# A two-layer encoder: the memory attention's transposes one unit later, with eight buffers of probabilities instead of four

## The chip, the cores and the metric

The kernel runs on one core of one Trainium2 chip. The metric is the device time of one execution in microseconds. The core has five engines that take their own instruction queues in order: PE (TensorE, matrix products and transposes), DVE (VectorE), ACT (ScalarE), POOL (GpSimd) and SP, which here only issues transfers. PEld is PE's weight load.

## What is computed

An encoder of two layers over 1024 positions of width 1024, in float32. Each layer has a mixing half with three groups and a gated feed-forward half. The change sits in the third group, attention of four heads of width 64 to 256 memory rows:

```python
def _memory_attn(q, km, vm):
    scores = jnp.einsum('bshd,bmhd->bhsm', q, km) * (HEAD_DIM ** -0.5)
    probs = jax.nn.softmax(scores, axis=-1)
    return jnp.einsum('bhsm,bmhd->bshd', probs, vm)

# in each layer
y = concat([rmsnorm(y_fourier), rmsnorm(y_window), rmsnorm(y_memory)]) @ w_out
x = x + rmsnorm(y)
gate, up = split(rmsnorm(x) @ w_ffn_in)
x = x + rmsnorm((silu(gate) * up) @ w_ffn_out)
```

## The kernel before, in words

**Precision.** Most products are made of float32 operands that are split in a high and a low part, and three products of the parts (`Acc.add`, L160). A split is a cast on ACT (L151) and a subtraction on DVE or POOL (L152).

**Memory attention** works in eight units, one per head and half of the sequence (512 positions). `mem_scores` (L828) multiplies queries and keys into two PSUM tiles `ms` (L839); DVE takes the row maximum (L841) and scales it (L842), ACT takes the exponential (L845) into a buffer of the ring `ems` and sums it, DVE takes the reciprocal of the sums (L849, tile `rden`), and POOL scales the probabilities in place (L851). `mem_turn` (L856) transposes them on PE into `mpT` (L861) and splits them into the ring `mps`, whose two buffers hold one unit. `mem_values` (L867) multiplies them with the values into `mav` (L872) and folds the two halves (ACT L875, DVE L876) into `ym`. One unit takes two buffers of `ems`, so its four buffers (at 16, 18, 20 and 22 of the float32 arena) hold two units.

**The order as written** (`mem_units`, L878): step i makes the scores of unit i, the values of unit i - 2 and the transposes of unit i - 1. The steps are woven by `weave` with the last query tiles (`q`, products `qp`, rotation L637, L639 on DVE and L642 on POOL; `q_turn`, transposes `qT`, split L379, L380).

**What follows it in each layer.** `fm_units` (L942) multiplies the Fourier and memory parts of each position tile with their rows of `w_out` (products `mo` from `big`). It first needs `group_scale` (L916): squares on ACT (L921) into the ring `sqs` at 16 and 18, a sum over partitions on PE (`ssp`, L924), L926 on DVE, L928 on POOL; only then can ACT and DVE empty its PSUM banks (L967, L969), of which there are two. It is woven with the first group of the window attention: scores `sc` (L727), DVE L728, exponential L740, POOL scaling L751, transposes `pT` (L764), values `av` (L779), folded into `ya` at 8 to 15 (L800, L801). Beside these, `load_wout` splits `w_out` (ACT L909, DVE L910). After that come the second group, `out` (products `mo` from `arena_r`, L1007, the norms L322 to L325 and L289), the transposes `hTp` (L1032) and the feed-forward products `qy`, `qz`, `qx`, `qw` (L1103), whose weight sums DVE makes in L1093.

**What sets the order.** The calls above are not the order of the queues. The program's builder runs its own scheduler over them (`schedule_with_timeline_sim=True` in `kernel`), which keeps data dependences and buffer reuse, and writes one in-order queue per engine. So a change of the written order changes the queues wherever the scheduler then decides otherwise.

Of the kernel before, what the change touches and what calls it, by code (L numbers as in the profile page):

```python
# [68 lines left out]
def tile_encoder(ctx: ExitStack, tc: tile.TileContext, T, C, out):  # L69
# [30 lines left out]
    def at(k, *shape, dt=F32):  # L100

        o = int(k * 256)
        ap = arenas[F32R if dt is F32R else F32][:, o : o + math.prod(shape)]
        return shaped(ap.bitcast(dt) if dt is I32 else ap, shape)
# [16 lines left out]
    def run(k, n, step):  # L121
        return Ring(*[k + i * step for i in range(n)])
# [2 lines left out]
    raws, junks = run(0, 3, 2), Ring(56)  # L125
    yfs, turns, kvs, ds = run(8, 2, 1), Ring(32, 34), Ring(10, 56, 58), run(12, 2, 2)
    ropes = {2: run(6, 4, 0.5), 8: run(36, 6, 2)}
    ems, es_ring, y1s = run(16, 4, 2), run(33, 5, 3), run(6, 2, 1)
    sqs, pms, xfs = run(16, 2, 2), run(20, 2, 2), Ring(16, 20, 24, 28, 32, 0)
    qws, sns, silus, acts = Ring(32, 0, 16, 20), Ring(36, 38, 40, 42, 32, 34), run(8, 5, 2), run(18, 7, 2)  # L130
    sums, wsums = run(8, 4, 2), Ring(4, 6)
# [327 lines left out]
    class Mix:  # L459
# [418 lines left out]
        def mem_units(self):  # L878
            todo = [(h, half) for half in range(2) for h in range(4)]
            st, pp = {}, {}  # L880
            n = len(todo)

            def unit(i):
                if i < n:
                    st[i] = self.mem_scores(*todo[i])
                if i >= 2:
                    h, half = todo[i - 2]
                    if h == 0 and half == 0:
                        ym = at(24, 2, 2, 512)
                        self.ym = [ym[:, i] for i in range(2)]  # L890
                    self.mem_values(h, half, pp.pop(i - 2))
                if 1 <= i <= n:
                    pp[i - 1] = self.mem_turn(st.pop(i - 1))

            return [lambda i=i: unit(i) for i in range(n + 2)]


        def load_wout(self, ks, k0=None):
# [424 lines left out]
    for l in range(DEPTH):  # L1323
# [57 lines left out]
        st = {}  # L1381
# [85 lines left out]
```

## Time and profile before

| | us |
|---|---|
| median of 3 runs (lowest to highest) | 2129.55 (2124.32 to 2131.04) |
| the profiled execution: its own time | 2127.03 |
| its span, first to last instruction | 2125.2 |
| PE busy | 2008.2 (94%) |
| DVE busy | 1594.6 (75%) |
| ACT busy | 1068.3 (50%) |
| POOL busy | 862.9 (41%) |

The span is the profiled execution without some 2 us around it. The shares are means over stages: the feed-forward half is nearly all PE, and what PE loses it loses in short stretches. The memory attention lies at about 139 to 224 us in layer 0 and 1185 to 1266 us in layer 1, the feed-forward half starts at about 406 and 1447 us.

### The profile page before, as it was taken

The numbers are of one execution on the slowest core, as the hardware profiler recorded it, in microseconds if no ns is written. First come the engines' busy times: TensorE is split into PE (matmuls) and PEld (weight loads), VectorE is DVE, ScalarE is ACT, GpSimd is POOL, SyncE is SP. The second block draws the span as 40 slices with busy tenths as digits, with TensorE's granted clock in tenths as the row PEclk, the third lists the DMA queues.
The fourth block names the chain that finished last, engine by engine and source line by source line (L and its number), as shares of the span: only waits on it lengthen the run. The fifth ranks groups of instructions, "written<-read, shape, count | busy, mean of one in ns | idle before, by whom it ended". The sixth has DMA issues, their size and how long they took to land. (4 is left out here: it accounts for less than half of the span.)

```text
span 2125.2 us, 28513 instructions
## 1 busy us (share of the span) xinstructions
PE 2008.2 (94%) x9586; PEld 1655.2 (78%) x9586; DVE 1594.6 (75%) x2445; ACT 1068.3 (50%) x2269; POOL 862.9 (41%) x858
## 2 busy tenths in 40 slices
PE   7998999699999999999899979997999999989997
PEld 6886787488888887888778868775888888877885
DVE  7568666998877877667967686669887877877674
ACT  6477767553333334444545676775333333345441
POOL 4234437643423434321544444576443423432222
PEclk9999999899999999999999989998999999999998
DMA  6112122422332326987721122142332332389872
GB/s 222 45 50 65 65 95 106 152 65 95 122 100 94 111 95 193 352 270 263 257 84 45 49 70 99 67 143 95 104 109 95 119 100 93 119 290 328 278 229 79
DMA packets 173603, 287.52 MB, mean 135 GB/s; under 512 B 15480, under 2 KB 73360, under 8 KB 173456
## 3 DMA queue, kind: packets, MB, share of 16 engines
q1 hardware_dynamic: 165392, 266.82, 37.9%
q10 hardware_dynamic: 8064, 18.88, 2.3%
q8 instruction: 75, 1.23, 0.2%
q14 instruction: 72, 0.59, 0.1%
HBM read 219.06 MB, written 66.58 MB: 134 GB/s over the span
## 5 line engine op out<-in xcount | busy, mean ns | idle before, releaser
L151 ACT CAST arena_r<-arena_f 128x512 fp32r<-128x512 f32 (+1 forms) x780 | 444.6, 592 | 679.8 <-PE qz L1103 116.4
L152 DVE TENSOR_TENSOR arena_r<-arena_f,arena_r 128x512 fp32r<-128x512 f32 x676 | 545.2, 829 | 173.8 <-ACT arena_r L151 170.2
L1234 PE MATMUL fo<-arena_r 128*128 128x512 f32 x1848 | 437.5, 398 | 28.4 <-ACT arena_r L151 15.2
L1234 PEld LDWEIGHTS fo<-arena_r 128*128 128x128 f32 x1848 | 354.1, 193 | 106.9 <-ACT arena_r L151 17.8
L1103 PE MATMUL qy<-arena_r 128*128 128x512 f32 x1056 | 264.0, 399 | 27.8 <-ACT arena_r L151 22.9
L1103 PEld LDWEIGHTS qy<-arena_r 128*128 128x128 f32 x1056 | 202.7, 193 | 73.6 <-ACT arena_r L151 24.0
L1093 DVE TENSOR_TENSOR arena_f<-arena_f 128x512 f32<-128x512 f32 x220 | 204.6, 933 | 5.1
L1103 PE MATMUL qz<-arena_r 128*128 128x512 f32 x704 | 196.0, 389 | 0.2 <-DVE arena_r L152 0.2
L1123 POOL TENSOR_TENSOR arena_f<-arena_f 128x512 f32<-128x512 f32 x44 | 73.1, 1660 | 294.5 <-ACT arena_f L1108 294.5
L1215 POOL TENSOR_TENSOR arena_f<-arena_f 128x512 f32<-128x512 f32 x50 | 72.5, 1454 | 229.4 <-DMA arena_f<-in_w_ffn_out 145.0
L1103 PEld LDWEIGHTS qz<-arena_r 128*128 128x128 f32 x704 | 132.0, 188 | 28.0 <-DVE arena_r L152 0.7
L1155 POOL TENSOR_TENSOR arena_f<-arena_f 128x512 f32<-128x512 f32 x44 | 73.5, 1672 | 173.4 <-DVE arena_f L1135 126.3
L152 POOL TENSOR_TENSOR arena_r<-arena_f,arena_r 128x256 fp32r<-128x256 f32 (+2 forms) x104 | 84.1, 813 | 126.9 <-ACT arena_r L151 95.0
L1103 PE MATMUL qw<-arena_r 128*128 128x512 f32 x528 | 127.6, 389 | 0.8 <-ACT arena_r L151 0.8
L1103 PE MATMUL qx<-arena_r 128*128 128x512 f32 x528 | 127.7, 389 | 0.5 <-ACT arena_r L151 0.5
L1103 PE MATMUL qx<-big,arena_r 128*128 128x512 f32 x528 | 127.0, 389 | 0.0
L1103 PEld LDWEIGHTS qw<-arena_r 128*128 128x128 f32 x528 | 99.1, 188 | 21.8 <-ACT arena_r L151 1.2
L1103 PEld LDWEIGHTS qx<-arena_r 128*128 128x128 f32 x528 | 99.1, 188 | 21.4 <-ACT arena_r L151 0.9
L1103 PE MATMUL qz<-big,arena_r 128*128 128x512 f32 x352 | 115.5, 389 | 0.0
L1103 PEld LDWEIGHTS qx<-big,arena_r 128*128 128x128 f32 x528 | 99.1, 188 | 20.5
L162 PE MATMUL mo<-arena_r 128*128 128x512 f32 x384 | 102.2, 403 | 3.2 <-DVE arena_f L1007 3.2
L162 PE MATMUL mo<-big,arena_r 128*128 128x512 f32 x384 | 102.9, 407 | 0.3 <-ACT arena_f L967 0.3
(225 smaller groups left out, 3570.6 us busy)
## 6 DMA issues: line engine op xcount, KB each, us to landing
arena_f<-in_w_ffn_out SPq DMA_DIRECT2D x264, 256.0 KB, 4.3
arena_f<-in_w_ffn_in SPq DMA_DIRECT2D x88, 512.0 KB, 3.6
actd<-arena_f SPq DMA_DIRECT2D x154, 256.0 KB, 3.7
arena_f<-actd SPq DMA_DIRECT2D x154, 256.0 KB, 4.1
arena_f<-in_w_in SPq DMA_DIRECT2D x40, 256.0 KB, 2.7
arena_f<-in_x SPq DMA_DIRECT2D x16, 512.0 KB, 5.0
arena_f<-in_w_out SPq DMA_DIRECT2D x32, 256.0 KB, 2.7
pmd<-arena_f ACTq DMA_DIRECT2D x32, 256.0 KB, 2.0
```

Source lines behind the costliest of these rows:

```text
L151: nc.scalar.copy(hi, src)
L152: return (lo_eng or nc.vector).tensor_tensor(out=lo, in0=src, in1=f32(hi), op=ALU.subtract)
L162: mm(self.dst, a, b, start=self.i == 0, stop=self.i == self.n - 1)
L1093: nc.vector.tensor_tensor(out=s, in0=a, in1=b, op=op)
L1103: mm(pt, a, b, start=start and n == 0, stop=n == 11, skip_group_check=not start)
L1123: nc.gpsimd.tensor_tensor(out=self.v, in0=self.v, in1=self.s2, op=ALU.add)
L1155: (G if i in (0, 3) else V).tensor_tensor(out=a[i], in0=c, in1=g[i], op=ALU.mult)
L1215: (nc.vector, nc.gpsimd)[k % 2].tensor_tensor(out=s, in0=x, in1=y, op=op)
L1234: mm(pt, ab[:, 0, x, sl], ab[:, 1, y], start=new and first and j == 0, stop=last and j == 2, skip_group_check=not new)
```

## The change

The transposes of a unit are called two steps behind its scores instead of one, its values three instead of two, and `ems` gets four more buffers, at 8, 10, 12 and 14. There are eleven steps instead of ten, so `weave` mixes them a little differently with the query tiles.

```diff
-    ems, es_ring, y1s = run(16, 4, 2), run(33, 5, 3), run(6, 2, 1)
+    ems, es_ring, y1s = Ring(16, 18, 20, 22, 8, 10, 12, 14), run(33, 5, 3), run(6, 2, 1)
...
             def unit(i):
                 if i < n:
                     st[i] = self.mem_scores(*todo[i])
-                if i >= 2:
-                    h, half = todo[i - 2]
-                    if h == 0 and half == 0:
+                if i >= 3:
+                    h, half = todo[i - 3]
+                    if i == 3:
                         ym = at(24, 2, 2, 512)
                         self.ym = [ym[:, i] for i in range(2)]
-                    self.mem_values(h, half, pp.pop(i - 2))
-                if 1 <= i <= n:
-                    pp[i - 1] = self.mem_turn(st.pop(i - 1))
+                    self.mem_values(h, half, pp.pop(i - 3))
+                if 2 <= i < n + 2:
+                    pp[i - 2] = self.mem_turn(st.pop(i - 2))
 
-            return [lambda i=i: unit(i) for i in range(n + 2)]
+            return [lambda i=i: unit(i) for i in range(n + 3)]
```

Lines behind L884 stand one further down in the changed kernel. No instruction is added or taken away; the queues of all engines are permuted between the memory attention and the first feed-forward products of each layer, and are equal elsewhere. Three places follow, as they stand in the built programs.

**PE, layer 0, behind the memory attention**, from a sum over partitions on. `mav_2108` is the last unit's values, `sc` and `pT` belong to the window attention, and `mo_2187` is the product of `fm_units` that follows its first two. Before:

```order
L924 MATMUL ssp_2312<-const,arena_f 128x2 x2
L779 MATMUL av_2216<-arena_r 128x512
L764 MATMUL pT_2320<-const,arena_f 128x128 x4
L727 MATMUL sc_2476<-arena_r 128x384 x2
L764 MATMUL pT_2329<-const,arena_f 128x128 x4
L764 MATMUL pT_2338<-const,arena_f 128x128 x4
L162 MATMUL mo_2187<-big_2064,arena_r 128x512 x3
L162 MATMUL mo_2187<-big_2071,arena_r 128x512 x3
L727 MATMUL sc_2576<-arena_r 128x384 x2
```

Now:

```order
L925 MATMUL ssp_2157<-const,arena_f 128x2 x2
L872 MATMUL mav_2108<-arena_r 128x512
L727 MATMUL sc_2252<-arena_r 128x384 x2
L727 MATMUL sc_2352<-arena_r 128x384 x2
L925 MATMUL ssp_2209<-const,arena_f 128x2 x2
L727 MATMUL sc_2356<-arena_r 128x384 x2
L727 MATMUL sc_2360<-arena_r 128x384 x2
L162 MATMUL mo_2187<-big_2043,arena_r 128x512 x3
L162 MATMUL mo_2187<-big_2050,arena_r 128x512 x3
L727 MATMUL sc_2364<-arena_r 128x384 x2
L764 MATMUL pT_2217<-const,arena_f 128x128
```

The product `mo_2187` stood behind 18 transposes `pT`, four `av` and five pairs of `sc` that follow the last `mav`; now it stands ahead of the first `pT`, and the transposes come among the products.

**DVE, layer 1, around the reciprocal of the fourth unit** (`rden_10210` before, `rden_10189` now). L637 and L639 rotate the last query tile. Before:

```order
L842 TENSOR_SCALAR nmx_10190<-rmax_10189 128x2
L380 TENSOR_TENSOR arena_r<-qT_10265,arena_r 64x4x128
L910 SCALAR_TENSOR_TENSOR big_10510<-arena_f,const,big_10510 128x512
L876 TENSOR_TENSOR arena_f<-mav_10216,arena_f 64x512
L152 TENSOR_TENSOR arena_r<-mpT_10230,arena_r 128x512
L637 TENSOR_TENSOR arena_f<-qp_10370,const 128x512
L639 TENSOR_TENSOR arena_f<-qp_10370,const 128x512
L841 TENSOR_REDUCE rmax_10274<-ms_10277 128x2
L849 RECIPROCAL rden_10210<-den_10191 128x4
```

Now:

```order
L911 SCALAR_TENSOR_TENSOR big_10489<-arena_f,const,big_10489 128x512
L152 TENSOR_TENSOR arena_r<-mpT_10250,arena_r 128x512
L849 RECIPROCAL rden_10189<-den_10170 128x4
L876 TENSOR_TENSOR arena_f<-mav_10243,arena_f 64x512
L152 TENSOR_TENSOR arena_r<-mpT_10257,arena_r 128x512
L637 TENSOR_TENSOR arena_f<-qp_10349,const 128x512
L639 TENSOR_TENSOR arena_f<-qp_10349,const 128x512
L911 SCALAR_TENSOR_TENSOR big_10489<-arena_f,const,big_10489 128x512
L841 TENSOR_REDUCE rmax_10216<-ms_10219 128x2
L380 TENSOR_TENSOR arena_r<-qT_10292,arena_r 64x4x128
```

The reciprocal moved ahead of the rotation, and one split of `w_out` (L910, now L911) and one split of `qT` (L380) moved behind it. On POOL the scaling of this unit stands behind the rotation's last step, L642, in both.

**DVE, layer 0, where the feed-forward half starts.** L1093 (now L1094) is the first sum of feed-forward weights. Before:

```order
L324 SCALAR_TENSOR_TENSOR arena_f<-arena_f,rrs_3984 128x1024
L1050 TENSOR_TENSOR arena_f<-big_3511,big_3504 128x512
L1050 TENSOR_TENSOR arena_f<-big_3504,big_4003 128x512
L1007 SCALAR_TENSOR_TENSOR arena_f<-mo_4025,grs_3950,arena_f 128x512
L152 TENSOR_TENSOR arena_r<-big_4003,arena_r 128x4x128
L1007 SCALAR_TENSOR_TENSOR arena_f<-mo_4039,grs_3950,arena_f 128x512
L152 TENSOR_TENSOR arena_r<-arena_f,arena_r 128x4x128
L1093 TENSOR_TENSOR arena_f<-arena_f 128x512
```

Now:

```order
L1008 SCALAR_TENSOR_TENSOR arena_f<-mo_4039,grs_3950,arena_f 128x512
L289 SCALAR_TENSOR_TENSOR arena_f<-arena_f,nrs_3993 128x1024
L324 SCALAR_TENSOR_TENSOR arena_f<-arena_f,rrs_4057 128x1024
L1051 TENSOR_TENSOR arena_f<-big_3504,big_4003 128x512
L152 TENSOR_TENSOR arena_r<-big_4003,arena_r 128x4x128
L1064 TENSOR_TENSOR big_3996<-big_3996,big_4003 128x4x128
L325 TENSOR_TENSOR arena_f<-arena_f 128x1024
L152 TENSOR_TENSOR arena_r<-arena_f,arena_r 128x4x128
L1094 TENSOR_TENSOR arena_f<-arena_f 128x512
```

Five more instructions of DVE now stand ahead of the first weight sum: one each of L289, L324, L325, L152 and L1063. They stood behind it before.

## Rows read from the trace of the kernel before

**Rows 1.** Busy time by stretch, layer 0; PEclk is the granted clock's share.

```profile
183.00:203.00 20.00, 14.50 (x65) 11.10 (x64) 19.26 (x33) 16.45 (x41) 8.14 (x13) 0.83 0.40 128
203.00:224.00 21.00, 15.02 (x81) 11.54 (x80) 17.96 (x49) 15.78 (x45) 9.44 (x17) 0.92 0.08 26
224.00:235.00 11.00, 9.79 (x47) 8.43 (x46) 5.98 (x24) 9.17 (x27) 5.21 (x9) 0.73 0.01 1
...
241.00:350.00 109.00, 108.72 (x604) 88.98 (x603) 67.21 (x186) 72.54 (x192) 52.64 (x83) 1.00 0.28 98
...
397.00:431.00 34.00, 17.56 (x63) 12.74 (x62) 32.78 (x41) 16.35 (x29) 16.04 (x13) 0.70 0.39 123
```

**Rows 2.** The same view, layer 1.

```profile
1229.00:1258.00 29.00, 20.58 (x93) 14.44 (x92) 27.35 (x49) 23.31 (x60) 15.43 (x21) 0.86 0.30 95
1258.00:1272.00 14.00, 11.24 (x56) 9.09 (x55) 10.46 (x35) 10.27 (x28) 3.10 (x7) 0.87 0.00 1
```

**Rows 3.** PE in order of time, layer 0: start, duration, instruction, idle and releaser.

```profile
216.83 0.71 PE L861 MATMUL mpT<-const,arena_f 128*128 128x128 f32 x5
...
224.46 0.51 PE L924 MATMUL ssp<-const,arena_f 128*128 128x2 f32 x4
...
232.97 1.91 PE L764 MATMUL pT<-const,arena_f 128*128 128x128 f32 x8
234.53 2.28 PE L162 MATMUL mo<-big,arena_r 128*128 128x512 f32 x6
```

**Rows 4.** ACT in order of time, layer 0.

```profile
212.64 0.42 ACT L921 ACTIVATE arena_f<-arena_f 128x256 f32<-128x256 f32 x1 [0.61 <-PE mpT L861]
...
230.97 0.67 ACT L967 ACTIVATE arena_f<-mo,grs 128x512 f32<-128x512 f32 x1
...
232.06 0.37 ACT L800 COPY arena_f<-av 64x256 f32<-64x256 f32 x1
```

**Rows 5.** PE in order of time at full clock, layer 0.

```profile
249.50 0.60 PE L764 MATMUL pT<-const,arena_f 128*128 128x128 f32 x4
249.85 0.48 PE L779 MATMUL av<-arena_r 128*128 128x512 f32 x1
250.17 1.55 PE L162 MATMUL mo<-big,arena_r 128*128 128x512 f32 x6
...
258.45 0.50 PE L924 MATMUL ssp<-const,arena_f 128*128 128x2 f32 x4
258.81 1.00 PE L727 MATMUL sc<-arena_r 128*128 128x384 f32 x4
```

**Rows 6.** PE in order of time, layer 1: the longest stall in the memory attention.

```profile
1234.41 1.85 PE L861 MATMUL mpT<-const,arena_f 128*128 128x128 f32 x8 [2.45 <-POOL arena_f L851]
```

**Rows 7.** POOL in order of time, just ahead of that stall.

```profile
1232.18 1.27 POOL L642 TENSOR_TENSOR arena_f<-arena_f 128x512 f32<-128x512 f32 x1 [7.03 <-DVE arena_f L639]
1233.43 2.29 POOL L851 TENSOR_SCALAR arena_f<-arena_f,rden 128x256 f32<-128x256 f32 x4
```

**Rows 8.** DVE in order of time, the same place.

```profile
1227.86 0.68 DVE L380 TENSOR_TENSOR arena_r<-qT,arena_r 64x512 fp32r<-64x512 f32 x1
1228.58 0.75 DVE L910 SCALAR_TENSOR_TENSOR big<-arena_f,const,big 128x512 fp32r<-128x512 f32 x1
...
1230.76 0.68 DVE L637 TENSOR_TENSOR arena_f<-qp,const 128x512 f32<-128x512 f32 x1
1231.36 0.68 DVE L639 TENSOR_TENSOR arena_f<-qp,const 128x512 f32<-128x512 f32 x1
```

**Rows 9.** DVE in order of time, layer 0, the feed-forward half's start.

```profile
404.99 0.68 DVE L1093 TENSOR_TENSOR arena_f<-arena_f 128x512 f32<-128x512 f32 x1
...
409.08 1.27 DVE L289 SCALAR_TENSOR_TENSOR arena_f<-arena_f,nrs 128x1024 f32<-128x1024 f32 x1
...
410.88 1.27 DVE L324 SCALAR_TENSOR_TENSOR arena_f<-arena_f,rrs 128x1024 f32<-128x1024 f32 x1
...
412.67 1.21 DVE L325 TENSOR_TENSOR arena_f<-arena_f 128x1024 f32<-128x1024 f32 x1
```

**Rows 10.** PE in order of time, layer 0, its first feed-forward product.

```profile
406.38 1.22 PE L1103 MATMUL qy<-arena_r 128*128 128x512 f32 x2 [8.88 <-ACT arena_r L151]
```

## The prediction

> **What bounds the kernel now.** I read the page's slices first, for where PE falls below nine tenths, and then the busy times of the four main engines in those stretches. In layer 0 PE is busy 14.50 of 20 us from 183 on, 15.02 of the next 21 and 9.79 of the next 11, and the granted clock falls to 0.83, 0.92 and 0.73 of full speed, that is, part of the time stands at the lower of its two levels [rows 1]. In layer 1 it is busy 20.58 of 29 us and 11.24 of 14 [rows 2]. Idle PE time in these stretches sums to 12.7 us in layer 0 and 11.2 us in layer 1; busy time multiplied by the missing share of the clock gives 6.3 and 4.3 us more. That is 34.5 us, the ceiling of anything that a change to the memory attention can return.
>
> The column beside it says why so little of it is free. DVE is busy 19.26 of the first 20 us, 17.96 of the next 21, and in layer 1 27.35 of 29 [rows 1, 2]. It splits transposed probabilities, takes maxima and splits `w_out` all at once. PE's gaps there are DVE's work seen from the other side; a new order can only return what DVE idles: 0.7 and 3.0 us in layer 0, then 5.0 us from 224 to 235, and 1.7 and 3.5 us in layer 1.
>
> From 241 us on PE is full at full clock for 109 us, with DVE at 67.21 [rows 1]. So time won before 241 us is kept until the feed-forward half starts. There DVE binds again, 32.78 of 34 us, while PE is busy 17.56 [rows 1].
>
> **The change part by part.** The written delay is mostly not what changes. In the built programs PE takes the transposes of a unit behind the scores of the next one both before and now: the scheduler had already moved them. The pairs of units, their counts and the products that PE has issued are the same until the memory attention's last third in layer 0, and nearly so in layer 1. What changes is where the neighbours stand.
>
> *The four buffers, and their new places.* They add no instruction. Two things could wait for them. The first write of `ya`, which now overlaps the last two units' probabilities, must follow their transposes: those start last at 216.83, the write comes at 232.06, 15 us of cover [rows 3, 4]. If the cover went, DVE's first fold and the first `y` split would be late next, and PE would have `mo` to do. The other direction is the gain: the squares for the first position tile reuse buffers 16 and 18, and at 212.64 they waited for PE's transposes [rows 4]. With eight buffers these places are left by the fifth unit and not by the seventh. I cost the buffers at nothing and book their gain with the next item.
>
> *Layer 0, 183 to 224 us.* The same products in nearly the same order against a DVE that idles 3.7 us. I take 1.5 us: the fourth unit's reciprocal and its scaling come a few instructions earlier, and one or two score maxima move behind the point where PE resumes `mo`. Ends: nothing, and 3.7 us.
>
> *Layer 0, 224 to 235 us, the largest term.* The first sum over partitions stood at 224.46, so ACT could empty the first `mo` bank only at 230.97, and `mo` resumed at 234.53 [rows 3, 4]. Between, PE had 18 transposes, 4 `av`, 3 sums and 5 pairs of `sc`. At full clock these cost 0.35 us per four transposes, 0.32 per `av`, 0.36 per sum and at most 0.50 per pair [rows 5]: 1.6 + 1.3 + 1.1 + 2.5 = 6.5 us, in 10.1 us of time. So 3.6 us were lost to waits for POOL's and DVE's small steps and to the lower clock; eight transposes alone took 1.91 us there [rows 3]. Now the sums stand ahead of these, and `mo`, which waits for none of this, stands ahead of and among the transposes. I take 3.0 of the 3.6 us. Ends: a loss of 1, if the sums still come late on POOL, and 4.5, if the clock also recovers earlier before 241.
>
> *Layer 1.* The longest stall is 2.45 us, transposes of the fourth unit that wait for POOL's scaling [rows 6]. The reciprocal now stands five instructions of DVE earlier, some 3.4 us by the durations of 0.68 to 0.75. But POOL's queue has the rotation's last step, L642, ahead of the scaling, before and now, and L642 waited for DVE's L639 [rows 7, 8]. So the scaling can come earlier only as L639 does: by the L910 and the L380 that moved behind it, 0.75 + 0.68 = 1.4 us [rows 8]. I take 1.5 us for the whole layer, since here `mo` resumes at much the same place as before. Ends: a loss of 1, and the 5.2 us that DVE idles.
>
> *The start of the feed-forward half.* In layer 0 five instructions of DVE move ahead of the first weight sum: 1.27 + 1.27 + 1.21 for L289, L324 and L325, and L152 and L1063 at 0.68 each like L1093 [rows 9], together 5.1 us. The first product waited 8.88 us for the casts behind that sum [rows 10], so it will come later by up to that much; but the five are then done, the last tiles' transposes come sooner, and the products that follow wait less. DVE is full either way. I take zero. Ends: 1.2 us gained, what DVE idles there, and 5.1 lost. The transfers of `x`, `pmd` and the weights keep their number and, in pairs, their order; nothing is booked for them.
>
> *A rule against this reading.* The row shows DVE at 19.26 of 20 us in PE's bubbles [rows 1]. The Trainium skill (Perfetto Trace Analysis, Optimization Strategy) says that a gap which repeats on the engine that should be full can mean too few buffers for the next tile. By the rows the sum stays as it is; by that rule the eight buffers would close the gaps, which is the third rival.
>
> **The sum:** 1.5 + 3.0 + 1.5 + 0 = 6.0 us. The profiled execution took 2127.03 us, so 2121.0 us. It lies 2.5 us under the median of the three runs, 2129.55, whose spread is 6.7 us; I keep 2121.0. For this kernel 0.3% (6.4 us, about what a measurement can tell from no change) puts the bounds at 2123.2 and 2135.9.
>
> **The rivals.** *DVE gives nothing back.* For: it is full in three of the five stretches and full again at the feed-forward start, where an earlier arrival only meets DVE's own backlog. Against: PE is full for 109 us between, with DVE at 62%, so DVE has time to catch up. Then only a part of the second term stays: about 2 us, 2125 to 2131.
>
> *Slower: the later first weight sum in layer 0.* The five instructions delay the first feed-forward product by 5.1 us, PE stands idle longer, and its clock, already 0.70 there [rows 1], returns later: at that level 17.56 us of busy time lose 5.3 us now, and half as much again is 2.6. With nothing won upstream that is 2127.0 + 7.7 = 2134.7, with a little lost there 2137. It decides if the products that follow the first do not wait less than before by as much as the first waits more. For: DVE has 1.2 us of slack in 34. Against: the same five must be done for those products in any order.
>
> *The buffers were the limit.* If scores could run ahead and fill PE, as the rule has it, half the ceiling of 34.5 us would come back: 2110. Against: the number of score products ahead of the transposes is unchanged in the queue.
>
> *The change doesn't do what it says.* As to the written delay this is so already, and it is in the sum; with no side effect at all it is the first rival.
>
> **How the numbers follow.** The forecast gets 0.53 (2114 to 2125), DVE's backlog 0.29, the slower case 0.13, the buffers 0.05. Of the forecast 0.43 lies below 2123.2 and 0.10 above; with the third rival that makes 0.48 faster; 0.10 and 0.29 with 0.01 of the slower case make 0.40 the same, and 0.12 slower. The range leaves out the buffers and about half of the slower case: 2112 to 2135. The ends of the four terms, -3.7 to 0, -4.5 to 1, -5.2 to 1 and -1.2 to 5.1, reach 2112.4 and 2134.1, so it takes them in.
>
> **What would show it.** In the changed profile the second square's wait should end far before 212, the first emptied `mo` bank should come before 226 in layer 0, and PE should be busy over 10 of the 11 us from 224 at a clock of 0.85 or more, with the same products done some 4 us earlier at 241. In layer 1 the stall of 2.45 us should shrink to about 1. The first feed-forward product of layer 0 should wait longer than 8.88 us, and the ones behind it less. I am wrong if the layer-0 gain before 241 is under 2 us, or if PE's last feed-forward transposes come later than before by more than was won.

## The result, and the profile after

| | before | after |
|---|---|---|
| median, us (runs) | 2127.39 (12) | 2134.81 (12) |
| lowest to highest | 2124.32 to 2131.04 | 2131.45 to 2138.94 |
| the profiled execution | 2127.03 | 2134.53 |

The ratio is 1.0033, with a 95% interval of 1.0024 to 1.0042: the change costs 7.4 us. The forecast was 6.0 us less than before. All twelve runs of the kernel after lie above the slowest run of before.

From the page of the kernel after, the engines' busy times (share of the span, instructions):

```profile
PE 2007.6 (94%) x9586; PEld 1653.5 (78%) x9586; DVE 1598.3 (75%) x2445; ACT 1064.2 (50%) x2269; POOL 851.2 (40%) x858
```

PE's busy time is 0.6 us less than before and the span 7.5 us longer (2132.7), so all of the loss is idle time of PE. The stretches of [rows 1], in the kernel after (window, us, then each engine's busy time, PEclk, DMA share, GB/s):

```profile
183.00:203.00 20.00, 15.13 (x66) 11.30 (x65) 17.42 (x30) 15.20 (x38) 7.62 (x11) 0.74 0.41 133
203.00:224.00 21.00, 16.45 (x74) 11.17 (x73) 17.99 (x45) 16.36 (x44) 5.76 (x11) 0.87 0.12 37
224.00:235.00 11.00, 11.00 (x49) 9.49 (x48) 7.42 (x26) 7.54 (x21) 7.32 (x13) 0.79 0.14 50
241.00:350.00 109.00, 107.88 (x604) 87.99 (x602) 69.06 (x192) 73.36 (x198) 53.34 (x80) 1.00 0.27 95
397.00:431.00 34.00, 16.26 (x61) 12.72 (x61) 30.34 (x34) 16.40 (x30) 14.08 (x13) 0.70 0.42 139
```

In the first three stretches PE idles 4.87 + 4.55 + 0 = 9.4 us, where it idled 12.7. The granted clock is lower in the first two. Busy time multiplied by its missing share is 3.93 + 2.14 + 2.31 = 8.4 us, where it was 6.3. So in this execution 3.3 us of gaps are closed, and the lower clock costs 2.1 us more. How much of this another execution would show is told in the section on the prediction.

The stretches of [rows 2], moved by 3 us, since the memory attention of layer 1 starts 3.3 us later (its first scores at 1188.36 against 1185.06):

```profile
1232.00:1261.00 29.00, 19.08 (x93) 15.35 (x93) 26.71 (x48) 23.88 (x59) 10.48 (x18) 0.80 0.30 93
1261.00:1275.00 14.00, 11.17 (x57) 8.21 (x57) 10.92 (x34) 8.81 (x25) 3.70 (x9) 0.93 0.00 1
```

Here nothing is won: PE idles 9.92 + 2.83 = 12.8 us instead of 11.2, and busy time by missing clock is 4.6 us instead of 4.3.

PE in order of time in the kernel after (start, duration, instruction, idle and releaser), beside [rows 3], [rows 6] and [rows 10]:

```profile
226.91 2.40 PE L162 MATMUL mo<-big,arena_r 128*128 128x512 f32 x6
...
229.50 0.38 PE L764 MATMUL pT<-const,arena_f 128*128 128x128 f32 x2
...
401.47 1.94 PE L1033 MATMUL hTp<-const,arena_f 128*128 128x128 f32 x8 [6.14 <-DVE arena_f L289]
412.56 1.22 PE L1104 MATMUL qy<-arena_r 128*128 128x512 f32 x2 [9.14 <-ACT arena_r L151]
...
422.30 5.07 PE L1104 MATMUL qy<-arena_r 128*128 128x512 f32 x14 [4.07 <-ACT arena_f L1109]
...
1239.72 2.07 PE L872 MATMUL mav<-arena_r 128*128 128x512 f32 x4 [3.18 <-DVE arena_r L152]
...
1245.52 1.14 PE L861 MATMUL mpT<-const,arena_f 128*128 128x128 f32 x4 [2.87 <-POOL arena_f L851]
```

`mo` resumes at 226.91 and not at 234.53, ahead of the transposes `pT`, as read from the queues. At the start of the feed-forward half PE waits 6.14 us for the transposes of a late position tile, then 9.14 for the first weights. From 385 to 431 us it idles 19.4 us, all in the three idles shown; before it idled 17.9 us there, 8.88 of them in one piece. In layer 1 the longest stalls of the memory attention were 2.45 and 1.75 us, now they are 3.18 and 2.87.

To see where the 7.4 us are lost, take one instruction late in each layer's start, DVE's fourth difference of gated products (L1124, now L1125). Before:

```profile
489.60 0.69 DVE L1124 TENSOR_TENSOR arena_f<-qy,arena_f 128x512 f32<-128x512 f32 x1
...
1529.55 0.69 DVE L1124 TENSOR_TENSOR arena_f<-qy,arena_f 128x512 f32<-128x512 f32 x1
```

After:

```profile
492.59 0.69 DVE L1125 TENSOR_TENSOR arena_f<-qy,arena_f 128x512 f32<-128x512 f32 x1
...
1535.66 0.68 DVE L1125 TENSOR_TENSOR arena_f<-qy,arena_f 128x512 f32<-128x512 f32 x1
```

The first scores of layer 0 start at 139.13 before and 138.59 after, so layer 0 loses 2.99 + 0.54 = 3.5 us up to there. Layer 1 starts 3.30 us late and is 6.11 late at its landmark: 2.8 more. The last product ends 7.5 us late. These are two single executions; the last section shows that the landmark of layer 0 differs by 3 us and more between equal queues. The shares below therefore come from ratios of many runs.

### The profile page after: what moved, and what is told of

Its sections match the earlier page's. It is cut to its first block, busy times and chain, and to the rows that moved or that the text cites. A ratio compares the mean times of both kernels' runs of the same rounds, so it can differ in the third digit from the quotient of the medians.

```text
span 2132.7 us, 28503 instructions
## 1 busy us (share of the span) xinstructions
PE 2007.6 (94%) x9586; PEld 1653.5 (78%) x9586; DVE 1598.3 (75%) x2445; ACT 1064.2 (50%) x2269; POOL 851.2 (40%) x858
## 4 chain that ended last, share of the span: by engine, by line
PE 72%; DVE 10%; DMA 7%; ACT 4%; POOL 3%; issue 3%; SPq 0%; DVEq 0%; POOLq 0%; ACTq 0%
PE fo L1235 12%; PE qz L1104 11%; PE qx L1104 11%; PE qy L1104 10%; PE mo L162 6%; PE qw L1104 5%; DVE arena_r L152 4%; PE kvp L162 4%; PE qp L162 3%; DMA arena_f<-actd 3%; DMA arena_f<-in_w_ffn_out 2%; PE pT L764 2%; PE sc L727 2%; ACT arena_r L151 1%; PE zT L162 1%
## 5 line engine op out<-in xcount | busy, mean ns | idle before, releaser
L152 DVE TENSOR_TENSOR arena_r<-arena_f,arena_r 128x512 fp32r<-128x512 f32 x676 | 545.3, 828 | 182.4 <-ACT arena_r L151 179.6
L1104 PEld LDWEIGHTS qy<-arena_r 128*128 128x128 f32 x1056 | 201.2, 191 | 70.8 <-ACT arena_r L151 17.9
L1094 DVE TENSOR_TENSOR arena_f<-arena_f 128x512 f32<-128x512 f32 x220 | 206.1, 939 | 8.9 <-DMA arena_f<-in_w_ffn_in 3.9
L1124 POOL TENSOR_TENSOR arena_f<-arena_f 128x512 f32<-128x512 f32 x44 | 73.2, 1662 | 298.8 <-ACT arena_f L1109 298.8
L152 POOL TENSOR_TENSOR arena_r<-arena_f,arena_r 128x256 fp32r<-128x256 f32 (+2 forms) x104 | 85.2, 824 | 115.3 <-ACT arena_r L151 71.8
```

What stands on the lines that cost most here:

```text
L152: return (lo_eng or nc.vector).tensor_tensor(out=lo, in0=src, in1=f32(hi), op=ALU.subtract)
L1094: nc.vector.tensor_tensor(out=s, in0=a, in1=b, op=op)
L1104: mm(pt, a, b, start=start and n == 0, stop=n == 11, skip_group_check=not start)
L1124: nc.gpsimd.tensor_tensor(out=self.v, in0=self.v, in1=self.s2, op=ALU.add)
```

## The experiments

All are built from one of the two kernels. Some hold a part of the queues in a chosen order, with edges between instructions that wait for nothing and only tell the scheduler what comes first:

```diff
         tile_encoder(tc, T, C, out)
+        by = {i.name: i for i in nc.cur_bb.bb.instructions}
+        dep = mybir.DependencyInfo(mybir.DependencyClass.NoSync, mybir.DependencyReason.DATA)
+        for names in ROWS:
+            for x, y in zip(names, names[1:]):
+                tc.add_manual_dep(by[y], x, dep, reason="order")
```

`ROWS` holds the instructions' names for each engine in the order wanted. In the diffs below M(l) is the memory attention of layer l and what is woven with it up to `out_gains`; R(l) is what follows, up to the first feed-forward products. R consists of rows(l), the second group of the window attention and the output rows, and entry(l), the block sums, the first weight sums and products, and the last three position tiles' transposes. R(before, 0) is R of layer 0 in the order of the kernel before, and turn3_rest_as_before is the first run below. Medians are of 5 to 12 runs, and a ratio is to the runs of the kernel before on the same chip.

**The memory attention alone, and the queues behind it alone.** First the change with R of both layers as before:

```diff
+ROWS = R(before, 0) + R(before, 1)
```

> The changed kernel, with every engine's queue held to the order of the kernel before from the gains of the output rows (behind the first half of the attention) to the end of each layer; the memory stage and the first half of the attention keep the changed order. Theory (the new memory order wins some 3 us, and what loses them and 7 more is the new order of the queues where the feed-forward starts): 2123 to 2126 us, ratio 0.998 to 0.9995, and the first qy of layer 0 no later than 406. Rival 1 (the new memory order is itself the loss): 2132 to 2136, as the changed kernel. Rival 2 (the feed-forward start is bound by VectorE's work and takes back any lead): 2126.5 to 2128.5, ratio 1.000.

Measured: 2123.66 us, 0.9986 [0.9976, 0.9997]. So the change to the memory attention itself does not cost anything; it may return up to 5 us. The 0.0047 between this and 1.0033, some 10 us, are the order of the queues, but not only of those behind: M(0) is that of the kernel after, while M(1), which was not held, has another order here (PE's queues differ from 1252 us on). The runs on one layer below take the two apart.

The opposite, the kernel before with R as the scheduler made it for the kernel after:

```diff
+ROWS = R(after, 0) + R(after, 1)
```

> The mirror: the kernel before, with the queues held to the order of the changed kernel from the gains of the output rows to the end of each layer; its memory stage keeps its own order. Theory: 2131 to 2136, ratio 1.002 to 1.004, with the first qy of layer 0 at 412 or later. Rival 1: 2126 to 2129. Rival 2: 2127 to 2130.

Measured: 2139.56 us, 1.0059 [1.0046, 1.0072]. The order behind the memory attention costs by itself, here 12.5 us. Why it is more than the 10 above is not shown; M(1) is not quite that of the kernel before either (PE's queues differ from 1252 to 1296 us).

**Written order and buffers apart**, both with R as before. The later transposes with the four old buffers; the scores of a unit then overwrite the probabilities of the unit two back before these are transposed, so the attention's values change:

```diff
-    ems = Ring(16, 18, 20, 22, 8, 10, 12, 14)
+    ems = run(16, 4, 2)
...
+ROWS = R(before, 0) + R(before, 1)
```

> The three units of distance with the four old probability buffers, the rest of each layer held to the order of the kernel before. Theory (the gain in the memory stage is that products of the Fourier and memory rows move ahead, which needs no buffers): 2123 to 2127. Rival (the eight buffers carry the gain): 2127 to 2131, with the scores waiting for the transposes of four units back.

Measured: 2136.16 us, 1.0042 [1.0029, 1.0054]. The later transposes without their buffers lose 9 us. Since a unit's transposes must here follow the scores of the unit two on, which lie in the same place, the run does not price the order alone.

The kernel before with eight buffers:

```diff
-    ems, es_ring, y1s = run(16, 4, 2), run(33, 5, 3), run(6, 2, 1)
+    ems, es_ring, y1s = Ring(16, 18, 20, 22, 8, 10, 12, 14), run(33, 5, 3), run(6, 2, 1)
...
+ROWS = R(before, 0) + R(before, 1)
```

> Eight buffers with the old distance of two units, the rest of each layer held to the order of the kernel before. Theory: 2126 to 2129, ratio 1.000: the scores never waited for a buffer. Rival (the eight buffers carry the gain): 2122 to 2125.

Measured: 2125.77 us, 0.9995 [0.9986, 1.0003]. Four more buffers bring at most 3 us by themselves, together with what the scheduler made of them (PE's queue differs from that of the kernel before from 214 to 300 and from 1257 to 1347 us). They are what the later transposes need, not a gain of their own.

**One layer alone.** The change in layer 1 only, with its M left to the scheduler, which then found another order for it than in the run above:

```diff
+            d = 3 if self.l == 1 else 2
+            ems.i, ems.ks = 0, (16, 18, 20, 22, 8, 10, 12, 14) if self.l == 1 else (16, 18, 20, 22)
...
-                if i >= 2:
-                    h, half = todo[i - 2]
+                if i >= d:
+                    h, half = todo[i - d]
...
+ROWS = R(before, 0) + R(before, 1)
```

> The change in layer 1's memory stage alone, every other queue as in the kernel before. Theory (with the rest held, the new memory order lost 0.75 us by the fourth difference of the feed-forward products in layer 0 and won 4.8 in layer 1): 2121 to 2123 us, ratio 0.9973 to 0.9985. Rival (the two layers share the 2.6 us): 2124 to 2126.

Measured: 2127.07 us, 0.9999 [0.9986, 1.0013]. Nothing won. I then held M(1) in the order that it had in the first run of this section:

```diff
+ROWS = M(before, 0) + R(before, 0) + M(turn3_rest_as_before, 1) + R(before, 1)
```

> The kernel before with the change in layer 1's memory stage alone, that stage in the order which it has in the kernel whose rest was held; every other queue as in the kernel before. If that order wins 4.5 us in layer 1, as its one trace had it: 2121 to 2123, ratio 0.9972 to 0.998. If that trace was a lucky one of the clock: 2125 to 2127, ratio 0.999 to 1.000.

Measured: 2122.11 us (2117.97 to 2126.45), 0.9973 [0.996, 0.9985]. This beats both kernels, by 5.7 us the one before. Its windows, beside [rows 2] (the same start within 0.3 us):

```profile
1229.00:1258.00 29.00, 18.95 (x100) 15.22 (x98) 26.74 (x50) 24.34 (x61) 11.82 (x19) 0.82 0.30 91
1258.00:1272.00 14.00, 13.35 (x69) 9.67 (x70) 11.81 (x41) 11.69 (x36) 5.64 (x12) 1.00 0.05 19
```

Its PE in order of time:

```profile
1235.96 2.07 PE L872 MATMUL mav<-arena_r 128*128 128x512 f32 x4 [3.19 <-DVE arena_r L152]
...
1267.77 0.44 PE L764 MATMUL pT<-const,arena_f 128*128 128x128 f32 x2 [0.28 <-POOL arena_f L751]
```

The kernel before has this first `pT` here:

```profile
1274.14 0.38 PE L764 MATMUL pT<-const,arena_f 128*128 128x128 f32 x2
```

The long stall is still there, 3.19 us, and so is the second, 2.88. What is won comes behind them: from 1258 on PE is busy 13.35 of 14 us at full clock, where it was 11.24 at 0.87, and the first `pT` comes 6.4 us earlier.

The same for layer 0 alone:

```diff
+            d = 3 if self.l == 0 else 2
...
+ROWS = M(turn3_rest_as_before, 0) + R(before, 0) + M(before, 1) + R(before, 1)
```

> The same in layer 0 alone. The prediction priced the two steps in layer 0 at 4.5 us together, which would be 2122, ratio 0.998; the trace with both layers changed showed no gain there (0.75 us later): 2126 to 2128, ratio 1.000 to 1.0006.

Measured: 2127.5 us, 1.0003 [0.9994, 1.0011]. In layer 0 the change returns nothing, at most 1.3 us.

**Which part of the later queues costs.** On the kernel after, R of layer 0 as before:

```diff
+ROWS = R(before, 0)
```

> The changed kernel with layer 0 alone held to the order of the kernel before from the gains of the output rows on; layer 1 and all else as in the changed kernel. Theory (the new order behind the memory stage costs 2.8 us in layer 0 and 6.5 in layer 1): 2131 to 2133, ratio 1.002 to 1.003. Rival (the loss is made in layer 0, by the first weight sum standing behind five more VectorE instructions): 2124 to 2127.

Measured: 2132.65 us, 1.0022 [1.0011, 1.0033]: 0.0011 better than after. Then layer 0 as after, with layer 1 as in the first run:

```diff
+ROWS = M(turn3_rest_as_before, 1) + R(before, 1)
```

> The changed kernel with layer 1 alone put in order, both of the last two edits together: its memory stage as in the kernel that took 0.9973, and everything from the gains of the output rows on as in the kernel before; layer 0 exactly as in the changed kernel. If the two halves of layer 1's order only pay together (each alone took 1.0042 and 1.0022), and layer 0 costs the 0.0011 measured for it: 2123 to 2127, ratio 0.998 to 0.9998. If the edits simply add: 2133 to 2136, ratio 1.003 to 1.004.

Measured: 2130.09 us, 1.0017 [1.0005, 1.003]. With after and the first run these make a square. R(0) as before gains 0.0011 where layer 1 is as after and 0.0031 (1.0017 to 0.9986) where it is not; layer 1's order gains 0.0016 and 0.0036. The means are 0.0021 and 0.0026, about 4.5 and 5.5 us. Each difference is uncertain by some 0.0016, from the two intervals. So both layers share the loss; that they help each other is not shown. The kept traces agree on layer 0. From its first scores to its landmark it takes 351.5 to 357.5 us in the seven that have the queues of the kernel after there, 354.3 in the mean. In the three with the new M(0) and R(0) as before it takes 347.5 to 351.0, 349.4 in the mean, and in the kernel before and the two others with its queues 347.2 to 350.5, 349.0 in the mean. So R(0) costs about 5 us, and the new M(0) wins nothing.

Layer 1's two parts apart, on the kernel after:

```diff
+ROWS = M(turn3_rest_as_before, 1) + R(after, 1)
```

> The changed kernel; in layer 1 the memory stage and the first half of the attention stand in the order that they have in the kernel whose rest was held (ratio 0.9986); everything else exactly as in the changed kernel. Theory A: 2132 to 2136. Theory B: 2127 to 2130, ratio 1.000 to 1.0015.

```diff
+ROWS = M(after, 1) + R(before, 1)
```

> The changed kernel with layer 1 held to the order of the kernel before from the gains of the output rows to its end; layer 0 and layer 1's memory stage and first half of the attention exactly as in the changed kernel. Theory A (layer 1 loses at the start of its feed-forward half): most of 7.7 us comes back, 2126 to 2129, ratio 0.9995 to 1.001. Theory B (layer 1 loses by the order that the scheduler gave to its memory stage and first half of the attention, where the kernel with everything behind held had another one and came 5.5 us earlier to its first pT): 2132 to 2135, ratio 1.0025 to 1.004.

Measured: 2132.82 us, 1.0022 [1.0012, 1.0033], and 2136.33 us, 1.0042 [1.0026, 1.0057]. The other order of M(1) gains 0.0011 with R(1) as after and 0.0025 (1.0042 to 1.0017) with R(1) as before, 0.0018 in the mean. R(1) as before costs 0.0009 in the one case and gains 0.0005 in the other. The means are each uncertain by some 0.0012. By these totals the order of M(1) costs layer 1 some 4 us, and that of R(1) nothing that they can tell. The traces do not bear out the second half. From first scores to landmark layer 1 takes 347.3 us in the kernel after, 345.9 with R(1) as before, 345.2 with the other M(1) and 340.2 with both; the kernel before takes 344.5, and 352.2 when R is as after. Each is one trace, but where traces have equal queues of PE in layer 1 they agree to 1.3 us. So both orders cost in layer 1, and their shares are not settled.

Smaller pieces, each on the kernel after:

```diff
+ROWS = entry(before, 0)
```

> The changed kernel; in layer 0 alone, the block sums, first weights, first products and transposes of rows 5 to 7 stand among themselves as in the kernel before; the output rows and all else as in the changed kernel. Theory (the first weight sum is late because its weights land in the place of row 5's tile, and row 5's normalisation ends late: the load was issued at 401.40 instead of 393.52): no gain, 2133 to 2137, first qy of layer 0 at 411 or later. Rival (five VectorE instructions put ahead of the first weight sum, as the prediction's second rival has it): 2130 to 2132, first qy at 408 or earlier.

```diff
+ROWS = entry(before, 1)
```

> The same edit in layer 1 alone. Theory (the fourth weight load waits for row 6's normalisation, 1453.58 instead of 1445.15, whose square stands on ScalarE behind casts that wait for block sums): part of layer 1's 6.5 us comes back, 2130 to 2134. Rival (all of it is the order of sums and products among themselves): 2127 to 2129. If nothing comes back: 2134 to 2136, and it is the order of the output rows.

```diff
+ROWS = rows(before, 1)
```

> The changed kernel; in layer 1 alone, the second half of the attention and the output rows stand among themselves as in the kernel before; block sums, first weights and first products, and all else, as in the changed kernel. Theory (the 7.7 us that layer 1 loses are in the order of the output rows: with layer 0 held the kernel took 1.0022 of before, with both held 0.9986): 2126 to 2130, ratio 0.9995 to 1.0015. Rival (neither order costs by itself, only the two together): 2133 to 2137.

And in layer 1 the second normalisation of output row 6 (L284 on ACT, L208 and L210 on POOL, L289 on DVE), moved ahead of the casts for block sums that it stood behind:

```diff
-ACT: ..., casts of L151 behind L1051, L284 (row 6), ...
+ACT: ..., L284 (row 6), casts of L151 behind L1051, ...
```

> The changed kernel with one step moved in layer 1: the second normalisation of row 6 (its square on ScalarE, two small steps on GpSimd, its scaling on VectorE) stands ahead of the casts and the group scale of row 7 that it stood behind; every other queue as in the changed kernel. Theory (the fourth weight load waits for this step and then blocks ScalarE's queue): the load issues some 4 us earlier, the stall of 4.88 us before the 14 qy matmuls of layer 1 shrinks to 2 or 3, and the time falls to 2130 to 2133. Rival (VectorE's total work is the bound there): 2134 to 2136.

Measured: 2135.19, 2136.28, 2135.22 and 2134.96 us; 1.0035 [1.0023, 1.0047], 1.0041 [1.0027, 1.0055], 1.0037 [1.0024, 1.005] and 1.0037 [1.0024, 1.005]. None moves the time. The first tells most: in it four of the five DVE instructions stand behind the first weight sum of layer 0 again (one L289 of 1.29 us stays ahead), and still the first product starts at 411.40, only 1.2 us earlier than in the kernel after. So these instructions ahead of L1093 are not by themselves the cause.

**The late weight load.** If not DVE's order, a transfer could be late. Transfers of `w_ffn_in` on SP's queue, kernel after:

```profile
380.69 0.38 SPq L1079 DMA_DIRECT2D arena_f<-in_w_ffn_in  x1
...
401.40 14.48 SPq L1079 DMA_DIRECT2D arena_f<-in_w_ffn_in  x7
```

Before, the second was issued at 393.52. It goes to place 0 of the arena, where output row 5 lies until L289 has normalised it, in the kernel before at 390.98. After, that comes later (DVE in order of time):

```profile
397.97 3.35 DVE L289 SCALAR_TENSOR_TENSOR arena_f<-arena_f,nrs 128x1024 f32<-128x1024 f32 x1 [0.44 <-POOL nrs L210]
...
411.18 0.68 DVE L1094 TENSOR_TENSOR arena_f<-arena_f 128x512 f32<-128x512 f32 x1
```

It ends at 401.3, just ahead of the transfer. The weight sum L1094 follows at 411.18, 6.2 us later than L1093 in [rows 9]. Part of the delay lies in L289 itself: it took 3.35 us, where the same instruction took 1.90 at 390.98 and 1.27 in [rows 9]. A step of POOL runs beside it for most of that time (POOL in order of time, kernel after):

```profile
397.91 2.33 POOL L325 TENSOR_TENSOR arena_f<-arena_f 128x1024 f32<-128x1024 f32 x1
```

No run takes the two apart, so that POOL slows it is not shown.

I gave the weights other places, so that they need not wait, first throughout, in the kernel after and in the one before:

```diff
-    qws, sns = Ring(32, 0, 16, 20), Ring(36, 38, 40, 42, 32, 34)
+    qws, sns = Ring(36, 40, 44, 16), Ring(32, 34, 0, 2, 40, 42)
...
-                qws.ks, wsums.ks = (44, 48, 52, 56), (4, 6, 0, 2)
+                qws.ks, wsums.ks = (48, 52, 56, 44), (4, 6, 36, 38)
```

> The changed kernel with the first three weight tiles of the feed-forward half in the places of the attention's probabilities instead of those of the output rows, so that three of the four first loads wait for no row; the small copies that stood there move to the rows' places, and the scheduler orders the queues anew. Theory (in the changed kernel the first products wait for weights that wait for a row's normalisation): first qy of layer 0 at 405 or earlier, 2121 to 2128. Rival (VectorE's work bounds the start whatever the weights do): 2132 to 2137.

> The same edit on the kernel before. Theory: its first qy waits for the same loads, less: 2120 to 2125, ratio 0.997 to 0.9995. Rival: 2126 to 2129, since there the sums stand ahead of the weights anyway.

Measured: 2144.08 us, 1.0078 [1.0064, 1.0093], and 2145.62 us, 1.0092 [1.0075, 1.0109]. The first product of layer 0 now starts at 406.09 in the first, but ahead of the products with `w_ffn_out` PE waits 8 to 10 us longer in each layer. PE at their start in the first of the two:

```profile
853.04 10.13 PE L1235 MATMUL fo<-arena_r 128*128 128x512 f32 x36 [11.81 <-ACT arena_r L151]
```

The same place in the kernel before:

```profile
846.44 18.24 PE L1234 MATMUL fo<-arena_r 128*128 128x512 f32 x72 [3.35 <-ACT arena_r L151]
```

PE waits 11.81 us where it waited 3.35, so the totals say nothing on the first weights. The trace of the second says something: its first product comes 256.6 us behind the first scores, 10.7 us sooner than in the kernel before, and its landmark at 350.4 us, where the kernel before has 350.5. An earlier first product alone has won nothing there. Then the other places only for the first two quads of weights:

```diff
-        qws.ks, wsums.ks = (32, 0, 16, 20), (4, 6)
+        qws.ks, wsums.ks = (36, 40, 16, 20), (4, 6)
+        sns.ks = (32, 34, 0, 2, 58, 56)
...
+                sns.ks = (36, 38, 40, 42, 32, 34)
```

> The changed kernel with new places for the first pair of quads alone: the gate's two weight tiles land in the attention's probabilities, which are free before row 5 ends, and the six small copies of that pair take the rows' places; from the second pair on the places are those of the changed kernel, so the second half's first loads (11.81 us of PE waiting in early_loads, 3.35 in the kernel before) should come when they did. Theory (the gate's second weight load, which waits for row 5, makes the first products late): first qy of layer 0 at 407 or earlier, and 2127 to 2131, ratio 1.000 to 1.002. Rival (VectorE's work bounds the start whenever the weights come): first qy earlier, later products as late as before, 2133 to 2137.

Measured: 2135.33 us, 1.0033 [1.0021, 1.0045]. PE at the start of the feed-forward half of layer 0:

```profile
405.34 1.97 PE L1033 MATMUL hTp<-const,arena_f 128*128 128x128 f32 x8 [8.99 <-DVE arena_f L289]
406.96 3.66 PE L1104 MATMUL qy<-arena_r 128*128 128x512 f32 x12
```

The 9.14 us ahead of the first product are gone, and the landmark of layer 0 lies at 491.17 from a start of 141.12, 4 us better than after, which is within the spread of equal queues. But the scheduler planned layer 1 anew, and from its first scores to its landmark that took 7 us longer than in the kernel after. So the late load does delay the first product of layer 0; what it costs layer 0 and the total was not separated.

## Why the prediction was wrong

**Buffers, zero: right.** The squares wait no more (ACT in order of time, kernel after; the first stood at 212.64 in [rows 4], the second at 213.87), and the first `mo` bank is emptied at 226.10 and not at 230.97, at about the 226 of the test:

```profile
196.72 0.41 ACT L922 ACTIVATE arena_f<-arena_f 128x256 f32<-128x256 f32 x1
...
198.67 0.41 ACT L922 ACTIVATE arena_f<-arena_f 128x256 f32<-128x256 f32 x1
...
226.10 0.69 ACT L968 ACTIVATE arena_f<-mo,grs 128x512 f32<-128x512 f32 x1
```

Both are worth nothing in time: the run with the buffers alone has them too (squares at 197.59 and 199.22, the bank at 226.93), and gave 0.9995. The third rival, that they were the limit, is refuted by the same run; the rule of the Trainium skill (Perfetto Trace Analysis, Optimization Strategy) did not describe these gaps.

**Layer 0, 4.5 us up to 235 us: wrong, the first step that failed.** The order did what was said, and PE is busy all 11 us from 224 on. The step took a closed gap to be time won ("I take 3.0 of the 3.6 us"), and time won before 241 us to be kept. In this trace 3.3 us of idle time are closed and 2.1 us of clock added. At 241 us PE has done 17 products `mo` more, and five `av`, three `sc` and one `pT` less: 2.0 us of work at the prices of [rows 5]. Its earlier start is 0.5 of that, which leaves 1.5, under the 2 us that I had set as the point where I am wrong. In the 109 us behind, PE now idles 1.1 us instead of 0.3. In total time the layer-0 change alone gave 1.0003, a gain of at most 1.3 us.

The clock's part in this is of two kinds. From 183 to 203 us it goes with the order: the granted clock is 0.74 to 0.76 in the thirteen kept traces that have the new M(0), and 0.83 in the five that have the old one, which is some 1.5 us more of busy time lost. PE idles less there, but in a longer piece (PE in order of time, before and after):

```profile
189.21 0.47 PE L872 MATMUL mav<-arena_r 128*128 128x512 f32 x1 [2.16 <-DVE arena_r L380]
189.50 1.31 PE L872 MATMUL mav<-arena_r 128*128 128x512 f32 x3 [3.01 <-DVE nmx L842]
```

From 203 us on it differs from execution to execution. I expected 0.85 or more from 224 to 235, and it was 0.79; but of two other runs with the same queues there, the one with the other M(1) and the one with R(1) as before, each on the kernel after, the first had 1.00 and the second 0.57 (PE busy, PEclk, DMA share, GB/s):

```profile
224.00:235.00 11.00, 10.52 (x58) 1.00 0.14 50
224.00:235.00 11.00, 11.00 (x41) 0.57 0.07 26
```

So the part of the 3.6 us that I read as lower clock was not the order's to give back: the old order's five traces, too, lie between 0.53 and 0.90 in this window. The Trainium skill (TensorE: Matmul & The Clock Gate, Why this matters for your kernels) advises to leave no long idle gaps between bursts of products, so that the clock does not drop. The trace agrees as far as it goes: the longest gap grew by 0.85 us, and the clock of that stretch fell, though the sum of the gaps did not grow.

**Layer 1, 1.5 us: mis-sized, and for the wrong reason.** The term came from a stall of 2.45 us, transposes behind POOL's scaling, that would shrink. The longest of that kind is now 2.87 us, and products `mav` wait 3.18 behind DVE; in the best run these are 2.88 and 3.19, so the stalls are not where the gain lies. What the change can return here is 5.7 us (0.9973), at about the end of 5.2 that I gave, and only in one of the three orders that the runs show. The scheduler's choice in the kernel after is another, and costs: 347.3 us up to the landmark, against 344.5 before and 340.1 in the best run. My lower end, a loss of 1 us, left out that the neighbours are reordered as well: holding that order back gave 0.0018, 4 us.

**The feed-forward start, zero: wrong, the second step that failed.** I had "DVE is full either way. I take zero". The first product waits longer, as said, 9.14 behind another 6.14 us, and what follows it waits 4.07 against 7.5 before, but PE's idle time from 385 to 431 us rose by 1.5 us, and its last transposes came 1.5 us later in layer 0 and 9 in layer 1, which had started 3.3 late. The order behind the memory attention of layer 0 costs 0.0021, some 4.5 us. This lies inside the bound of 5.1 that I gave it, and I chose the other end.

**The second rival** gave the right time, 2134.7 to 2137, and one right place. Its mechanism, five DVE instructions ahead of the first weight sum, is not it by itself: with four of them back behind the sum the time stays at 1.0035. And with the later queues of layer 0 put back the ratio is still 1.0022, so much of the loss is not in layer 0 at all. That its time came out is luck. The range held the time at its upper edge. Of 0.12 for slower, too little came from the reorder: the terms were priced for what a move could free, and what the scheduler moves elsewhere only at the feed-forward start, there at zero. What remains open is why the new order costs in each layer: the late load in layer 0 fits the trace, but was not isolated, and in layer 1 no single instruction was found.

## What to carry to other kernels

Where a scheduler writes the queues, a change of written order is two changes: the one meant, and a new order wherever the scheduler then decides otherwise. Hold the second with order edges and time the two apart; here one was worth -3 us and the other 10. Look in the queues which parts really stayed as they were: what is not held is planned anew, too. Do it for each layer or stage by itself, since the same edit gave 5.7 us in one layer and nothing in the other. And do not book closed PE gaps at full value where the granted clock of the stretch is already low, nor read its level there from one trace.

## What was not expected of the hardware

Two executions with the same queues can differ in where the low clock falls. The kernel before and the one with the change in layer 1 alone have the same order in layer 0. PE in three windows of layer 0 (busy time, PEclk, DMA share, GB/s), the kernel before:

```profile
220.00:225.00 5.00, 3.20 (x19) 1.00 0.00 0
225.00:230.00 5.00, 3.79 (x19) 0.91 0.02 3
230.00:235.00 5.00, 5.00 (x21) 0.50 0.00 0
```

The change in layer 1 alone, M(1) left to the scheduler:

```profile
220.00:225.00 5.00, 3.44 (x12) 0.77 0.00 0
225.00:230.00 5.00, 4.85 (x27) 0.89 0.01 3
230.00:235.00 5.00, 4.78 (x30) 1.00 0.00 0
```

From 230 on the one runs at 0.50, the lower level of 1.2 GHz, and the other at 2.4 GHz. The landmark of layer 0 lies at 489.60 from a start of 139.13 in the first and at 487.32 from 140.14 in the second: 3.3 us between equal queues. Of the seven traces with the queues of the kernel after in layer 0, the shortest takes 351.5 us from first scores to landmark and the longest 357.5. In layer 1 traces with equal queues of PE agree to 1.3 us. The Trainium skill (TensorE: Matmul & The Clock Gate, What's actually happening) says that the point at which the clock changes differs from run to run, since what the chip goes by does not start anew with the kernel. The two tables agree with that. A difference of a few us between two single traces of layer 0 is therefore not evidence for an edit.
